# A hybrid decoder step on one core: the input projection of token blocks 2 to 4 in products of 512 columns

## The chip, the core and the metric

The kernel runs on one core of a Trainium2 chip. The time is the device time of one execution in microseconds, the median of three runs. The core has five engines that run side by side and meet through semaphores: TensorE (PE, matrix products; its loads of the stationary operand are shown apart as PEld), VectorE (DVE), ScalarE (ACT), GpSimd (POOL) and SyncE (SP), which here only issues DMA transfers. A product holds one operand of up to 128x128 still in the array (the stationary one) and streams the other through it (the moving one); its result goes to a bank of PSUM, which holds 512 float32 columns for each of 128 partitions.

## The reference

One inference step of a layer with two groups of heads, for 2048 new prompt tokens and 8 sequences of 8 sample tokens. All of them share one input projection:

```python
z = jnp.einsum('bsd,dc->bsc', x, w_in)            # 1024 x 3600
fq, fk, fv = z[..., 0:512], z[..., 512:1024], z[..., 1024:1536]   # attention: queries, keys, values
qk_in = z[..., OFF_M_QK:OFF_M_V]                  # 1024 columns, short convolution of width 4, then silu
mv, ig, lf = values, input gate, forget gate      # matrix memory (mLSTM)
og = jax.nn.sigmoid(z[..., OFF_M_O:] + b_og)      # 512 columns, output gate
```

Behind it come a causal attention with forgetting over the prompt, an attention of the sample tokens over 8192 cached positions, the chunked recurrence of the matrix memory, an output projection with layer norm, and a squared-ReLU network with a second layer norm. (The lines above shorten the reference's; the order of the columns is its own.)

## The kernel before

Everything is float32 and split: an operand `a` becomes `ah` (rounded by ScalarE, `split_hi`, L154) and `al = a - ah` (by VectorE, `split_lo`, L157), and one product becomes three, `ah*bh + ah*bl + al*bh`, in `mm3` (L163 to L165). So every step over 128 rows of the inner dimension issues three matmuls, each with its own weight load.

The work has four parts in order of time: A (input projection, `block_a`), B (prompt attention), O (output projection) and C (the network). Part A goes through four blocks of tokens, `BLKS`: block 1 holds the 64 sample tokens and 4 tiles of 128 prompt tokens, blocks 2 to 4 hold 4 tiles (512 tokens) each. In the code they are `bi` 0 to 3. For a block the split tokens lie in four tiles, `xh0`/`xl0` for the first 256 tokens (320 in block 1) and `xh1`/`xl1` for the other 256.

The columns come in passes of 256 (`W_PASSES`), 14 a block. `wload` fetches a pass in two pieces of 128x1024, each four row groups of 128 rows by 256 columns, and splits them (tiles `wra`, then `whi` and `wlo`, four buffers of each kind of split piece). The passes of a block, in their order:

- 2 passes `natural`: mLSTM values (and in the second one the gates `ig`, `lf`). The tokens are stationary, the 256 weight columns move; for each of the tiles 8 row groups x 3 matmuls go into one bank `pm`, then `sink` empties it.
- 4 passes for the convolution's input. Weights are stationary, 128 columns at a time (`j`), and 256 tokens move; for each half `i` of the block a bank, then a ScalarE copy into half of `qi`. After both halves VectorE does the convolution.
- 2 passes `natural`: output gates, stored as `dog`.
- 4 passes for the attention's queries and keys, in the manner of the convolution's input, stored as `dq` and `k_prompt`.
- 2 passes `natural`: the attention's values, stored as `v_prompt`. Their hooks also load the next block's tokens (`x_load`), split its first tile (`x_turn`), or in block 4 start loads for part B (`begin_b`).

Beside these passes two other streams are worked in. `tick(us)` is called behind each product with a share of time; each 2.3 units (`PACE_M`) let one step of the matrix memory through (`gate_stream`, `m_block`, `m_sample`; tiles `mr`, `mg`, `mm`, `mn`), each 5.6 units (`PACE_A`) one step of the sample attention (tiles `sQ`, `sO`, `sT`). A `natural` product ticks 2.6, a product with 256 moving tokens 2.56. The final order on each engine is set by a list scheduler that places instructions by its own estimate of when they become ready, so code order is not machine order. Buffers are released by the last instruction that uses a tile; within one tile, waits go by the region that is read or written.

Of the kernel before, what the change touches and what calls it, by code (L numbers as in the profile page):

```python
# [52 lines left out]
def body(ctx, tc, I, O, stages):  # L53
# [99 lines left out]
    def split_hi(dst, src, scale=1.0):  # L153
        last["ACT"] = A.activation(dst, src, AF.Copy, scale=scale)  # L154
# [141 lines left out]

    xT = {}
# [19 lines left out]
    def x_turn(bi, t):  # L317

        blk, pre, off = geom(bi)
        i = int(off[t] >= pre + 256)  # L320
        if len(xT.setdefault(bi, [])) == i:
            w = 256 if i else 320
            xT[bi].append((pa.tile([128, 8, w], F32R, name=f"xh{i}"), pa.tile([128, 8, w], F32R, name=f"xl{i}")))
        n = tok_n(t)
        xn = xns.pop(t)[:, :8 * n].rearrange("p (k c) -> p k c", k=8)
        (xh, xl), s = xcol(bi, t)
        split_hi(xh[:, :, s], xn)
        split_lo(xl[:, :, s], xn, xh[:, :, s])

    def xcol(bi, t):  # L330

        blk, pre, off = geom(bi)
        o = off[t]
        i = int(o >= pre + 256)
        o -= i * (pre + 256)
        return xT[bi][i], slice(o, o + tok_n(t))

# [120 lines left out]
    def block_a(bi):  # L458
# [3 lines left out]
        def natural(sink, *cols, hook=None, after=None):  # L462
            wh, wl = W0.pop() if W0 else wload(*cols)
            for i, t in enumerate(blk):
                if hook:
                    hook(i)
                m = tok_n(t)
                ps = ppa.tile([128, 512], F32, name="pm", tag="pm", bufs=4)[:m, :wh[0].shape[1]]
                (xh, xl), s = xcol(bi, t)
                for k in range(8):  # L470
                    mm3(ps, xh[:, k, s], xl[:, k, s], wh[k], wl[k], k == 0, k == 7)
                sink(t, m, ps)
                if after:
                    after(i)
                tick(2.6)

        def stage(ps, m, n):
# [26 lines left out]
        for j in range(8):  # L504
# [5 lines left out]
            if pre:  # L510
                qs = pa.tile([128, 8, 11], F32, name="qs", bufs=2)
                V.tensor_copy(qs[:, :, 0:3], scT[:, j])
            for i in range(2):
                xh, xl = xT[bi][i]
                w = 256 + (pre if i == 0 else 0)
                ps = ppa.tile([128, 512], F32, name="pm", tag="pm", bufs=4)[:, :w]
                for k in range(8):
                    mm3(ps, wh[k][:, cs], wl[k][:, cs], xh[:, k, :w], xl[:, k, :w], k == 0, k == 7)
                tick(w * 0.01)
                if w == 320:  # L520
                    A.copy(qs[:, :, 3:11], ps[:, 0:64].rearrange("p (b t) -> p b t", t=8))
                A.copy(qi[:, 3 + i * 256:259 + i * 256], ps[:, w - 256:])
            V.tensor_copy(hist[:, j], qi[:, 512:515])
# [25 lines left out]
        yield 1  # L549
        for i in range(2):  # L550
            def sink(t, m, ps, i=i):
# [10 lines left out]
        for j in range(8):  # L562
# [6 lines left out]
            scale = 1.0 if c else 0.125  # L569
            for i in range(2):  # L570
                xh, xl = xT[bi][i]
                w = 256 + (pre if i == 0 else 0)
                ps = ppa.tile([128, 512], F32, name="pm", tag="pm", bufs=4)[:, :w]
                for k in range(8):
                    mm3(ps, wh[k][:, cs], wl[k][:, cs], xh[:, k, :w], xl[:, k, :w], k == 0, k == 7)
                tick(w * 0.01)
                if w == 320:
                    for a in range(4):
                        V.tensor_scalar(qr[:, :, (j % 2) * 4 + a], ps[a * 32:a * 32 + 32, 0:64].rearrange("p (b t) -> p b t", t=8), scale, None, op0=OP.mult)
# [4 lines left out]
                st = pa.tile([128, 256], F32, name="st", bufs=4)  # L584
                A.activation(st, ps[:, w - 256:], AF.Copy, scale=scale)
                a = t0 + i * 256
                SY.dma_start(O["k_prompt"][jj * 128:(jj + 1) * 128, a:a + 256] if c else dq[jj, :, a:a + 256], st)
# [3 lines left out]
        for i in range(2):  # L591
            def sink(t, m, ps, i=i):
                d = v_out(t)[:, i * 256:(i + 1) * 256]
                (A if bi == 3 and i == 1 else SY).dma_start(d, stage(ps, m, 256))

# [7 lines left out]

            def b_first(n, i=i):
                if i == 1 and n == 0:
                    begin_b()
            natural(sink, (1024 + i * 256, 256), hook=b_first if bi == 3 else turn_first)

# [1394 lines left out]
```

## Time and profile before

| | us |
|---|---|
| median of 3 runs (3210.70 to 3214.76) | 3212.57 |
| profiled execution, its own time | 3215.55 |
| its span, first to last instruction | 3213.8 |
| part A, blocks 2 to 4, in the span | about 206 to 878 |
| part B begins | about 880 |
| granted TensorE clock, mean | 0.99 |

The page gives busy times of the engines, the span in 40 slices, DMA queues, the chain that ended last, and the costliest groups of instructions. In the groups, "mean ns of one" is the time from an instruction's start to its modelled end; matmuls overlap, so the distance from start to start is shorter, and it has to be read from the timeline.

### The profile page before, as it was taken

The numbers are of one execution on the slowest core, as the hardware profiler recorded it, in microseconds if no ns is written. First come the engines' busy times: TensorE is split into PE (matmuls) and PEld (weight loads), VectorE is DVE, ScalarE is ACT, GpSimd is POOL, SyncE is SP. The second block draws the span as 40 slices with busy tenths as digits, with TensorE's granted clock in tenths as the row PEclk, the third lists the DMA queues.
The fourth block names the chain that finished last, engine by engine and source line by source line (L and its number), as shares of the span: only waits on it lengthen the run. The fifth ranks groups of instructions, "written<-read, shape, count | busy, mean of one in ns | idle before, by whom it ended". The sixth has DMA issues, their size and how long they took to land. (4 is left out here: it accounts for less than half of the span.)

```text
span 3213.8 us, 57419 instructions
## 1 busy us (share of the span) xinstructions
PE 3124.1 (97%) x21597; PEld 2538.6 (79%) x21597; DVE 2082.2 (65%) x5046; ACT 1446.8 (45%) x2678; POOL 910.1 (28%) x973
## 2 busy tenths in 40 slices
PE   9999999999999999999999999999999999899998
PEld 8998998998867677677777777777767777698886
DVE  6856556465488788534556568556675665766667
ACT  4343344334378677412444445343444444344442
POOL 0121323423333333376333323334333211000000
PEclk9999999999999999999999999999999999999999
DMA  5565766867676866687887869878879866643231
GB/s 190 151 211 166 264 218 226 273 219 260 219 251 186 193 168 145 214 297 259 308 292 271 308 237 322 317 256 313 291 260 340 288 210 204 211 163 131 100 123 63
DMA packets 339340, 732.75 MB, mean 228 GB/s; under 512 B 63608, under 2 KB 177656, under 8 KB 338168
## 3 DMA queue, kind: packets, MB, share of 16 engines
q1 hardware_dynamic: 251928, 414.61, 39.8%
q0 software_dynamic: 83520, 304.12, 27.1%
q10 hardware_dynamic: 3616, 10.36, 0.9%
q8 instruction: 171, 2.80, 0.3%
q14 instruction: 105, 0.86, 0.1%
HBM read 676.13 MB, written 86.38 MB: 237 GB/s over the span
## 5 line engine op out<-in xcount | busy, mean ns | idle before, releaser
L157 DVE TENSOR_TENSOR wl<-wr,wh 128x1024 fp32r<-128x1024 f32 x300 | 365.7, 1222 | 246.1 <-ACT wh L154 207.1
L154 ACT ACTIVATE wh<-wr 128x1024 fp32r<-128x1024 f32 x300 | 315.4, 1055 | 330.7 <-PE py L165 140.0
L163 PE MATMUL ph<-x1h,wh 128*128 128x512 f32 (+1 forms) x1280 | 455.2, 356 | 0.0
L164 PE MATMUL ph<-x1l,wh 128*128 128x512 f32 (+1 forms) x1280 | 453.5, 354 | 0.2 <-DVE x1l L157 0.2
L165 PE MATMUL ph<-x1h,wl 128*128 128x512 f32 (+1 forms) x1280 | 451.5, 355 | 0.4 <-DVE wl L157 0.2
L1720 POOL DMA_INDIRECT kT<-cache_k,idxK x256 | 276.4, 1080 | 533.7 <-PE sQ L1743 468.6
L163 PE MATMUL py<-wh,hh 128*128 128x512 f32 x900 | 358.8, 403 | 10.4 <-DVE y L1369 6.4
L164 PE MATMUL py<-wl,hh 128*128 128x512 f32 x900 | 354.4, 395 | 0.7 <-issue 0.7
L165 PE MATMUL py<-wh,hl 128*128 128x512 f32 x900 | 351.9, 395 | 0.7 <-DVE hl L157 0.4
L1369 DVE TENSOR_TENSOR y<-y,py 128x512 f32<-128x512 f32 x410 | 276.8, 681 | 106.5 <-PE py L165 80.3
L163 PE MATMUL pm<-xh,whi 128*128 128x256 f32 (+1 forms) x1024 | 298.5, 292 | 0.0
L164 PE MATMUL pm<-xl,whi 128*128 128x256 f32 (+1 forms) x1024 | 294.5, 288 | 0.0
L165 PE MATMUL pm<-xh,wlo 128*128 128x256 f32 (+1 forms) x1024 | 293.6, 287 | 0.5 <-issue 0.5
L1831 POOL DMA_INDIRECT vt<-cache_v,idxV x164 | 179.1, 1092 | 386.8 <-PE sO L1855 315.1
L163 PEld LDWEIGHTS ph<-x1h,wh 128*128 128x128 f32 x1280 | 241.2, 188 | 40.2 <-issue 8.5
L165 PEld LDWEIGHTS ph<-x1h,wl 128*128 128x128 f32 x1280 | 240.6, 189 | 36.7 <-issue 3.7
L164 PEld LDWEIGHTS ph<-x1l,wh 128*128 128x128 f32 x1280 | 241.5, 189 | 35.0 <-issue 3.7
L163 PE MATMUL pm<-whi,xh 128*128 128x256 f32 (+2 forms) x816 | 237.0, 291 | 9.8 <-ACT whi L154 7.2
L164 PE MATMUL pm<-wlo,xh 128*128 128x256 f32 (+2 forms) x816 | 232.6, 285 | 0.8 <-DVE wlo L157 0.6
L165 PE MATMUL pm<-whi,xl 128*128 128x256 f32 (+2 forms) x816 | 232.3, 285 | 0.8 <-issue 0.8
L163 PEld LDWEIGHTS py<-wh,hh 128*128 128x128 f32 x900 | 169.4, 189 | 65.2 <-issue 25.1
L157 DVE TENSOR_TENSOR wlo<-wra,whi 128x1024 fp32r<-128x1024 f32 (+1 forms) x112 | 141.6, 1266 | 102.0 <-ACT whi L154 95.5
(364 smaller groups left out, 6806.7 us busy)
## 6 DMA issues: line engine op xcount, KB each, us to landing
wr<-w SPq DMA_DIRECT2D x200, 512.0 KB
wra<-w_in SPq DMA_DIRECT2D x104, 512.0 KB
wr<-dw SPq DMA_DIRECT2D x96, 512.0 KB
dw<-w POOLq DMA_DIRECT2D x48, 512.0 KB
Rb<-dR SPq DMA_DIRECT2D x128, 128.0 KB
kT<-dw SPq DMA_DIRECT2D x28, 512.0 KB
kT<-w SPq DMA_DIRECT2D x25, 512.0 KB
xn<-xp_t SPq DMA_DIRECT2D x16, 512.0 KB
```

The source lines that it names most:

```text
L154: last["ACT"] = A.activation(dst, src, AF.Copy, scale=scale)
L157: r = (eng or V).tensor_tensor(dst, src, hi.bitcast(F32), op=OP.subtract)
L163: T.matmul(ps, wh, xh, start=first, stop=False, skip_group_check=shared)
L164: T.matmul(ps, wh, xl, start=False, stop=False, skip_group_check=shared)
L165: last["PE"] = T.matmul(ps, wl, xh, start=False, stop=stop, skip_group_check=shared)
L1369: V.tensor_tensor(y, y, ps, op=op)
L1720: G.indirect_dma_start(out=piece(n), out_offset=None, in_=ck, in_offset=IO(ap=idxK[:, b, j // 2, j % 2:j % 2 + 1], axis=0))
L1831: vx["last"] = G.indirect_dma_start(out=vt.rearrange("p f c -> p (f c)"), out_offset=None, in_=cv, in_offset=IO(ap=idxV[:, b, (kt % 4) * 4 ...
```

## The change

Block 1 and the first two passes of each block stay. In blocks 2 to 4:

- The split tokens lie in one pair of tiles, `xh` and `xl` of 128x4608. In blocks 2 to 4 each token tile has its own 1024 columns (8 row groups x 128 tokens), so that for a row group the 512 tokens of a block are four runs of 128 at a distance of 1024. Block 1 keeps its two parts, inside the same pair of tiles (`xcol`, `xrun`).
- The convolution's input and the queries and keys take 512 moving tokens in one product and one bank, instead of twice 256 (`xrun`, `pv`). One ScalarE copy of 512 columns fills `qi`; queries and keys are still stored as two pieces of 256. Such a product ticks 5.12.
- Output gates and values go through `wide`: 512 columns, which are two former passes, move past each stationary token tile. The weights come in four pieces of two row groups x 512 columns (the same bytes, fetched as two runs of 512 numbers a partition). For each piece all four tiles are worked, each into its own bank, so all four banks `pm` stay in use over the pass and are emptied with the last piece. Each group of six matmuls ticks 1.3. The sinks work on 512 columns, in buffers shared with the convolution's `ac` and `qi`.
- The hooks of the values' pass move with it (`at`): the next block's first three token tiles are loaded behind the first group of pieces 0 to 2, its first tile is split behind the first group of the last piece; `begin_b` comes behind the first group of piece 2.

```diff
     def x_turn(bi, t):
-        blk, pre, off = geom(bi)
-        i = int(off[t] >= pre + 256)
-        if len(xT.setdefault(bi, [])) == i:
-            w = 256 if i else 320
-            xT[bi].append((pa.tile([128, 8, w], F32R, name=f"xh{i}"), pa.tile([128, 8, w], F32R, name=f"xl{i}")))
+        if not XX:
+            XX.extend(pa.tile([128, 4608], F32R, name=x) for x in ("xh", "xl"))
...
     def xcol(bi, t):
         blk, pre, off = geom(bi)
+        if bi:
+            o = off[t] * 8
+            return [X[:, o:o + 1024].rearrange("p (k c) -> p k c", k=8) for X in XX]
...
+    def xrun(bi):
+        if bi:
+            return [(512, [X[:, 0:4096].rearrange("p (t k c) -> p k t c", t=4, k=8) for X in XX])]
+        return [(w, [X[:, a:a + 8 * w].rearrange("p (k c) -> p k c", k=8) for X in XX]) for a, w in ((0, 320), (2560, 256))]
...
+        def wide(sink, c0, hook=None):
+            banks = [ppa.tile([128, 512], F32, name="pm", tag="pm", bufs=4) for _ in blk]
+            at0, at1 = (w_at[((c0 + i * 256, 256),)] for i in range(2))
+            for q in range(4):
+                wr = pa.tile([128, 4 * 272], F32, name="wra", bufs=2)[:, :1024]
+                SY.dma_start(wr.rearrange("p (s e) -> p s e", s=2),
+                             dap(I["w_in"], at0 + q // 2 * 131072 + q % 2 * 512, [[1024, 128], [at1 - at0, 2], [1, 512]]))
+                wh = pa.tile([128, 4 * 272], F32R, name="whi", bufs=4)[:, :1024]
+                wl = pa.tile([128, 4 * 272], F32R, name="wlo", bufs=4)[:, :1024]
+                split_hi(wh, wr)
+                split_lo(wl, wr, wh)
+                wh, wl = (x.rearrange("p (s k c) -> p k s c", s=2, k=2) for x in (wh, wl))
+                for i, t in enumerate(blk):
+                    xh, xl = xcol(bi, t)
+                    for k in range(2):
+                        mm3(banks[i].rearrange("p (s c) -> p s c", s=2), xh[:, 2 * q + k], xl[:, 2 * q + k], wh[:, k], wl[:, k],
+                            q == k == 0, q == 3 and k == 1)
+                    if hook:
+                        hook(q, i)
+                    if q == 3:
+                        st = (pa.tile([128, 512], F32, name="sa", tag="ac", bufs=2) if i % 2 else
+                              pa.tile([128, 512], F32, name="sq", tag="qi", bufs=2))
+                        sink(t, banks[i], st)
+                    tick(1.3)
...
-            for i in range(2):
-                xh, xl = xT[bi][i]
-                w = 256 + (pre if i == 0 else 0)
+            at = 3
+            for w, (xh, xl) in xrun(bi):
                 ps = ppa.tile([128, 512], F32, name="pm", tag="pm", bufs=4)[:, :w]
+                pv = ps.rearrange("p (t c) -> p t c", t=4) if w == 512 else ps
                 for k in range(8):
-                    mm3(ps, wh[k][:, cs], wl[k][:, cs], xh[:, k, :w], xl[:, k, :w], k == 0, k == 7)
+                    mm3(pv, wh[k][:, cs], wl[k][:, cs], xh[:, k], xl[:, k], k == 0, k == 7)
                 tick(w * 0.01)
...
+        def gate_out(t, ps, st):
+            V.tensor_tensor(st, ps, bog, op=OP.add)
+            A.activation(st, st, AF.Tanh, scale=0.5)
+            V.scalar_tensor_tensor(st, st, 1.0, nwh, op0=OP.add, op1=OP.mult)
+            SY.dma_start(dog[t * 128:t * 128 + 128], st)
+        if bi:
+            wide(gate_out, C_O)
+        for i in range(0 if bi else 2):
...
+        def v_store(t, ps, st):
+            A.copy(st, ps)
+            (A if bi == 3 else SY).dma_start(v_out(t), st)
+
+        def at(q, i):
+            if bi == 3:
+                if (q, i) == (2, 0):
+                    begin_b()
+            elif q < 3 and i == 0:
+                x_load(BLKS[bi + 1][q])
+            elif (q, i) == (3, 0):
+                x_turn(bi + 1, BLKS[bi + 1][0])
+                x_load(BLKS[bi + 1][3])
+
+        if bi:
+            wide(v_store, 1024, at)
+        for i in range(0 if bi else 2):
```

Three places show what becomes of the order of instructions. In each row the line is `mm3`'s or the helper's; L7xx to L19xx move by 56 lines between the two files.

The first is TensorE at the output gates of block 2. Before, one bank (`pm_4188`, tile 4's first 256 columns) is worked through all eight row groups, and the weights change under it after four:

```order
L163 MATMUL pm_4188<-whi_4178,xh0_2987 128x256
L164 MATMUL pm_4188<-wlo_4179,xh0_2987 128x256
L165 MATMUL pm_4188<-whi_4178,xl0_2988 128x256
L163 MATMUL pm_4188<-whi_4184,xh0_2987 128x256
L164 MATMUL pm_4188<-wlo_4185,xh0_2987 128x256
L165 MATMUL pm_4188<-whi_4184,xl0_2988 128x256
```

Now one piece of weights (`whi_3968`) stays and the banks go by under it (the transposition `mm_3781` belongs to the matrix memory of the sample tokens):

```order
L163 MATMUL pm_3964<-whi_3968,xh_147 128x512
L164 MATMUL pm_3964<-wlo_3969,xh_147 128x512
L165 MATMUL pm_3964<-whi_3968,xl_148 128x512
L890 MATMUL mm_3781<-ident_74,hT_3730 64x128
L163 MATMUL pm_3965<-whi_3968,xh_147 128x512
L164 MATMUL pm_3965<-wlo_3969,xh_147 128x512
L165 MATMUL pm_3965<-whi_3968,xl_148 128x512
```

What moved: a bank is left after six matmuls of 512 columns instead of 24 of 256, and the order of weights and tiles has changed places. In all, TensorE's program has 16,675 instructions, where it had 18,403.

The second is TensorE in block 3, where `m_block` takes two steps (each fills one `mn` with two heads) beside the queries' products. Before, each step stands alone between two products of 24 matmuls; this is the second one, the first stands 24 matmuls earlier:

```order
L165 MATMUL pm_7355<-xh1_5701,wlo_7205 128x256
L719 MATMUL mn_7380<-va_6908,Wm_6911 128x129
L720 MATMUL mn_7380<-Cs_5966,qa_6913 128x129
L719 MATMUL mn_7380<-va_6908,Wm_6911 128x129
L720 MATMUL mn_7380<-Cs_5966,qa_6913 128x129
L163 MATMUL pm_7407<-xh0_5623,whi_7397 128x256
```

Now both steps stand side by side behind one product (and a step of the sample attention, `sO`, in the second of them):

```order
L775 MATMUL mn_6329<-va_6030,Wm_6033 128x129
L776 MATMUL mn_6329<-Cs_5316,qa_6035 128x129
L775 MATMUL mn_6340<-va_6030,Wm_6033 128x129
L776 MATMUL mn_6340<-Cs_5316,qa_6035 128x129
L775 MATMUL mn_6340<-va_6030,Wm_6033 128x129
L1911 MATMUL sO_5877<-vt_6111,PTs_5742 32x256 x4
L1911 MATMUL sO_5877<-vt_6109,PTs_5742 32x256 x4
L776 MATMUL mn_6340<-Cs_5316,qa_6035 128x129
L163 MATMUL pm_6379<-xh_147,whi_6369 128x512
```

What moved: a product ticks 5.12 at once, and two steps of 2.3 go through together. The numbers of steps are the same in both: 336 `sQ`, 170 `sO` and 62 `sT` matmul instructions stand ahead of part B in either program.

The third is the SP queue at the end of the values' pass of block 2. Before, stores of 256 columns stand between the fetches of weights (`wra`):

```order
L284 DMA wra<-w_in 128x1024
L594 DMA v_prompt<-st 128x256
L656 DMA Wm<-dM 128x4x128
L656 DMA qa<-dar 128x4x128
L594 DMA v_prompt<-st 128x256
L1727 DMA Rb<-dR 128x1x256 x2
L594 DMA v_prompt<-st 128x256
L664 DMA va<-dv 128x4x128
L704 DMA og<-dog 128x512
L594 DMA v_prompt<-st 128x256
L284 DMA wra<-w_in 128x1088 x2
```

Now:

```order
L284 DMA wra<-w_in 128x1088
L712 DMA Wm<-dM 128x4x128
L712 DMA qa<-dar 128x4x128
L284 DMA wra<-w_in 128x1024
L315 DMA xn<-xp_t 128x1024
L637 DMA v_prompt<-sq 128x512
L720 DMA va<-dv 128x4x128
L637 DMA v_prompt<-sa 128x512
L637 DMA v_prompt<-sq 128x512
L760 DMA og<-dog 128x512
L637 DMA v_prompt<-sa 128x512
```

What moved: the next pass's weights and the next block's last token tile (`xn`) stand ahead of all the stores, and there are four stores of 512 columns, all at the end.

More of the change, by code (lines that the diff above doesn't have):

```diff
@@ L521, in block_a @@
                     A.copy(qs[:, :, 3:11], ps[:, 0:64].rearrange("p (b t) -> p b t", t=8))
-                A.copy(qi[:, 3 + i * 256:259 + i * 256], ps[:, w - 256:])
+                n = w // 256 * 256
+                A.copy(qi[:, at:at + n], ps[:, w - n:])
+                at += n
             V.tensor_copy(hist[:, j], qi[:, 512:515])
@@ L583, in block_a @@
                         SY.dma_start(O["k_sample"][jj * 128:(jj + 1) * 128], st)
[L584 to L587, printed above, removed]
+                for o in range(w % 256, w, 256):
+                    st = pa.tile([128, 256], F32, name="st", bufs=4)
+                    A.activation(st, ps[:, o:o + 256], AF.Copy, scale=scale)
+                    SY.dma_start(O["k_prompt"][jj * 128:(jj + 1) * 128, a:a + 256] if c else dq[jj, :, a:a + 256], st)
+                    a += 256
             if pre and j % 2 == 1:
@@ L590, in block_a @@
         kx["new"] = True
-        for i in range(2):
+        def v_store(t, ps, st):
[13 more added lines that the diff above has]
+        for i in range(0 if bi else 2):
             def sink(t, m, ps, i=i):
-                d = v_out(t)[:, i * 256:(i + 1) * 256]
-                (A if bi == 3 and i == 1 else SY).dma_start(d, stage(ps, m, 256))
+                SY.dma_start(v_out(t)[:, i * 256:(i + 1) * 256], stage(ps, m, 256))
             def turn_first(n, i=i):
@@ L602, in turn_first @@
                     x_load(BLKS[bi + 1][3])
[L604 to L607, printed above, removed]
+            natural(sink, (1024 + i * 256, 256), hook=turn_first)
     dgs_s = drm.tile([4, 8], F32, name="dgs_s")
```

33 lines of the change are left out of this document (16 added, 17 removed).

## The prediction

> **What bounds the kernel now.** I read the page's engine rows first, then the stretch of blocks 2 to 4 in a view by windows, then TensorE's waits in it, then the timeline for the distance between matmuls.
>
> ```profile
> span 3213.8 us, 57419 instructions
> PE 3124.1 (97%) x21597; PEld 2538.6 (79%) x21597; DVE 2082.2 (65%) x5046; ACT 1446.8 (45%) x2678; POOL 910.1 (28%) x973
> 206.00:878.00 672.00, 661.54 (x5949) 616.05 (x5947) 381.28 (x1086) 251.38 (x536) 202.88 (x215) 1.00 0.69 229
> 206.00:878.00 672.00, 536.35 (x4187) 1.00 0.69 229
> PE sO L1855 <- DMA vt<-cache_v,idxV: 3.2, 2, 2.7
> PE sT L1792 <- ACT PTs L1814: 1.5, 1, 1.5
> PE pm L165 <- issue: 1.3, 3, 0.6
> PE sT L1812 <- ACT PTn L1794: 1.2, 1, 1.2
> PE mm L634 <- POOL va L663: 0.9, 1, 0.9
> ```
>
> TensorE is busy 97% of the span. In the stretch of blocks 2 to 4 (first window row: length, then busy time of PE, PEld, DVE, ACT, POOL, then granted clock, DMA share, GB/s) it is busy 661.54 of 672 us at clock 1.00; 536.35 us of that belong to the projection's products `pm` (second window row, `pm` alone). VectorE has 381 us and ScalarE 251 us, so neither bounds. The waits of TensorE there (us in total, times, longest) sum to some 8 us. So a change of this stretch is worth what it takes from TensorE's own stream.
>
> **What a matmul costs, narrow and wide.** A start-to-start distance is what counts. Two pieces of the timeline (start, duration), the first with 256 moving columns behind a step of the sample attention, the second in part C with 512 behind such a step:
>
> ```profile
> 857.11 1.05 PE L1855 MATMUL sO<-vt,PTs 128*32 128x256 f32 x16
> 858.08 0.39 PE L163 MATMUL pm<-whi,xh 128*128 128x256 f32 x1
> 858.31 0.28 PE L164 MATMUL pm<-wlo,xh 128*128 128x256 f32 x1
> ...
> 859.38 0.28 PE L164 MATMUL pm<-wlo,xh 128*128 128x256 f32 x1
> 1645.68 1.05 PE L1855 MATMUL sO<-vt,PTs 128*32 128x256 f32 x16
> 1646.66 0.50 PE L163 MATMUL py<-wh,hh 128*128 128x512 f32 x1
> 1647.00 0.40 PE L164 MATMUL py<-wl,hh 128*128 128x512 f32 x1
> ...
> 1649.10 0.39 PE L164 MATMUL py<-wl,hh 128*128 128x512 f32 x1
> ...
> 1657.26 0.39 PE L164 MATMUL py<-wl,hh 128*128 128x512 f32 x1
> 1649.00:1657.00 8.00, 8.00 (x37) 1.00 0.97 331
> 412.92 0.28 PE L164 MATMUL pm<-wlo,xh 128*128 128x256 f32 x1
> ...
> 415.44 0.28 PE L164 MATMUL pm<-wlo,xh 128*128 128x256 f32 x1
> ```
>
> Undisturbed: from 412.92 to 415.44 lie 21 steps (every third row is L164), 2.52/21 = 0.120 us for 256 columns. From 1649.10 to 1657.26 lie 36 steps (a multiple of three; the window counts 37 that touch its 8 us), 8.16/36 = 0.227 us for 512 columns. Two narrow ones take 0.240, so each pair that becomes one wide matmul saves 0.013 us. The columns take the same time either way; what goes is a fixed share of one matmul.
>
> The Trainium skill, "TensorE: Matmul & The Clock Gate", section "Back-to-back issue gap", gives a warm gap of N/2.4 + 2.5 ns, that is a fixed share of 2.5 ns; by it, as an estimate, the fixed share would save 1728 x 0.0025 = 4 us and the sum would be a loss of some 3 us. The trace doesn't agree: 0.120 us above, where the formula gives 0.109.
>
> Behind an interruption the first ten steps are dearer. Narrow: 858.08 to 859.38 is 1.30 us for ten, 0.10 over 1.20. Wide: 1646.66 to 1649.10 is 2.44 us, 0.17 over 2.27. So each entry costs 0.07 us more when the products are wide.
>
> **The sum.** Per block, 8 x 24 wide matmuls for the convolution's input, 96 for gates, 8 x 24 for queries and keys, 96 for values: 576, in three blocks 1728, where there were 3456.
>
> - Fixed share: 1728 x 0.013 = 22.5 us saved, all on TensorE and so on the path.
> - Entries: the built order has 98 places in blocks 2 to 4 where another stream's work is followed by a wide product; 98 x 0.07 = 6.9 us lost. (No cost if the entry were like the narrow one.)
> - Fewer interruptions: 109 entries into products where the order before has 123, since two matrix-memory steps now go together; 14 x 0.10 = 1.4 us saved.
> - Instruction supply: TensorE waits 1.3 us on "issue" at `pm` in these blocks, and now has 1728 matmuls and loads fewer to fetch. Worth 0 to 1.3; I take 0, since the quoted wait is 3 single cases.
> - Steps side by side: two steps of `m_block` with no product between them give VectorE, ScalarE and POOL less cover. Some 20 such pairs stand in the new order. The nearest row is the wait of `mm` on POOL, 0.9 us, once in 12 chunks before. Bounds 0 and 10 x 0.9 = 9 us, if every second pair waited like that; I take 1.5, since most pairs use buffers freed a product (5.4 us) earlier.
>
> 22.5 - 6.9 + 1.4 - 1.5 = 15.5 us. Against the profiled execution's 3215.55 us that is 3200; that one lies 3 us above the median, and against the median it is 3197.
>
> **What I cost at nothing, and its cover.**
>
> ```profile
> L157 DVE TENSOR_TENSOR wlo<-wra,whi 128x1024 fp32r<-128x1024 f32 x104 | 130.9, 1261 | 93.3 <-ACT whi L154 86.9 <-PE mn L720 2.7 <-PE pm L165 2.1
> L154 ACT ACTIVATE whi<-wra 128x1024 fp32r<-128x1024 f32 x104 | 109.0, 1057 | 82.9 <-PE pm L165 23.9 <-PE pm L164 23.2 <-DMA wra<-w_in 21.5
> L522 ACT COPY qi<-pm 128x256 f32<-128x256 f32 x64 | 22.8, 368 | 67.1 <-PE pm L165 59.3 <-DVE qk L535 3.2 <-remote 3.1
> L555 DVE TENSOR_TENSOR st<-pm,bog 128x256 f32<-128x256 f32 x32 | 13.3, 415 | 12.9 <-remote 4.8 <-PE pm L165 3.1 <-issue 2.7
> ```
>
> A weight piece in `wide` needs ScalarE 1.06 and VectorE 1.26 us and covers 24 matmuls, 5.45 us; four buffers let the splits run ahead, and a buffer is now free after each piece. Without that cover a piece would stop TensorE for 2.3 us. The fetch brings the same bytes in runs half as long; between the release of a buffer and the use of its next filling, the order leaves at least 4.3 us of products (3.8 before), by the distances above. Token tiles: the next block's first tile is split behind the first group of the last piece, with three groups (4.1 us) for 2.3 us of splitting; its readers in the old block are then done. Emptying a bank: twice 0.37 us (L522) or twice 0.42 (L555) become at most 0.84 in one; a bank is used again at least 4 us later. On SP, weights and token tiles are queued ahead of the stores, and the four wide stores end with the pass; `og` waits for `dog`, which is now complete only 4 us before the next product, but its use lies several steps on. POOL's gathers keep their number and order, with 2 to 3% less time between them: 3.2 us of waits on `vt` could become 5. At the change to part B the last `pm` matmul is still what VectorE's last state update waits for; the larger ScalarE copy adds 0.25 us beside that.
>
> **Rivals.**
>
> *The moving operand in runs costs.* Tokens now come in four runs of 128 (1152 matmuls), weights in two of 256 (576). If each of the 1152 x 3 + 576 = 4032 breaks cost as much as the fixed share of a matmul, 0.013 us, that would be 52 us, and the time 3212.6 + 52 - 15.5 = 3249. It decides from 15.5/4032 = 0.004 us a break. Against it:
>
> ```profile
> 855.36 1.93 PE L1743 MATMUL sQ<-kT,qb 128*32 128x256 f32 x32
> ```
>
> `sQ` moves two runs of 128, `sO` (the rows at 857.11 and 858.08 above) one of 256: from 855.36 to 857.11 it is 1.75/32 = 0.055 us a record, then 0.97/16 = 0.061 us. A break costs nothing there; it is plain float32 in a narrow array, so this isn't proof. 6%.
>
> *The waits take it.* Pairs of steps, gathers and the token splits stop TensorE for 9 us more than I allow: 3206 or a little over. For it: POOL and SP work in order, and one late gather holds `hh` and so the transposition. Against it: only 8 us of waits in 672 before. 12%.
>
> *Part B falls out otherwise.* The scheduler orders part B anew, though no line of it changes: TensorE's order differs from its first products on.
>
> ```profile
> PE pt L1019 <- ACT PT L1022: 5.8, 3, 3.0
> PE pS L974 <- DVE mx L982: 1.9, 3, 0.8
> 878.00:900.00 22.00, 15.92 (x72) 0.69 0.77 208
> ```
>
> Its waits sum to some 15 us from 880 to 1420, most in few places; one of 3 us more or less, at either sign, is within reach, and one low-clock window like the one at its begin (0.69 over 22 us) costs some 5. As a mechanism that alone gives no more than 3192 or 3203. 4% that it takes the time out of the range.
>
> *The clock gives way.* `wide` changes its bank every six matmuls of 512. If the granted clock sank to 0.69 there, as at the change to part B, 6 passes of 21.8 us would take 59 us more: 3256. But `py` in part C changes among its four banks every six matmuls of 512 too, and its window above has clock 1.00. The Trainium skill, "TensorE: Matmul & The Clock Gate", section "A second HAM failure mode: psum-queue depth-cycling", speaks of such oscillation at 512 columns with banks changing; by that rule this rival would hold, and the trace of part C doesn't agree. 2%.
>
> That the change would not do what it says is excluded: 1728 fewer TensorE instructions stand in the program.
>
> **How the numbers follow.** Forecast 76%, waits 12%, runs 6%, part B 4%, clock 2%. The likeliest case gives 3197. Its bounds: entries as before, no new wait and issue gained give 22.5 + 1.4 + 1.3 = 25, 3187; 9 us of waits in place of 1.5 give 3205, and part B's 3 us beside that 3207 or 3208. The range 3187 to 3207 holds the forecast and some of the waits' case. 0.2% is 6.4 us, about what a measurement can tell: faster means under 3206.1. The forecast, part B and half of the waits' case lie there, 86%; the other half of the waits' case is no change, 6%; runs and clock are slower, 8%.
>
> **What would show it.** In the changed profile, wide `pm` matmuls 0.227 us apart, blocks 2 to 4 shorter by about 15 us, the same clock, TensorE's waits there near 10 us, the distance behind an entry as in part C. Wrong if the distance of `pm` with four runs is over 0.231, if `mn`, `mm` or `sO` wait for tens of us, or if part B alone moves by more than 5 us.

## The result, and the profile after

The changed kernel is slower: 3227.42 us against 3215.0 us for the kernel before on the same chip (medians of 10 runs each), a ratio of 1.0045 with a 95% interval of 1.0034 to 1.0055. The forecast was 3197 us, some 15 us faster. So about 30 us are to be explained. The profiled execution took 3224.22 us, 3 us under its median; against the 3200 that were forecast for it, 24 us are to be explained there.

The page of the changed kernel, its span and engine rows:

```profile
span 3222.5 us, 53779 instructions
...
PE 3107.6 (96%) x19869; PEld 2444.2 (76%) x19869; DVE 2082.1 (65%) x5022; ACT 1439.0 (45%) x2630; POOL 906.0 (28%) x973
```

TensorE is 16.5 us less busy than before (3124.1), in a span 8.7 us longer. Where the time went is read from two windows of each kernel: from 200 us, inside the end of block 1, to the first product of part B (`pS`), and from there to the end. Columns: length, then busy time of PE, PEld, DVE, ACT, POOL, then clock, DMA share and GB/s. The kernel before:

```profile
200.00:880.40 680.40, 668.31 (x6003) 622.46 (x6002) 385.45 (x1096) 254.48 (x544) 207.00 (x222) 1.00 0.69 228
880.40:3213.80 2333.40, 2268.73 (x14146) 1731.98 (x14146) 1546.21 (x3462) 1117.60 (x1978) 676.26 (x712) 0.99 0.69 232
```

The changed kernel:

```profile
200.00:888.50 688.50, 661.70 (x4275) 532.24 (x4274) 382.80 (x1073) 245.95 (x500) 201.53 (x219) 0.99 0.67 225
888.50:3222.50 2334.00, 2258.68 (x14146) 1727.60 (x14146) 1549.96 (x3462) 1119.75 (x1978) 677.61 (x714) 0.99 0.69 232
```

Part B and what follows is as long as before (2334.0 against 2333.4), though TensorE is 10.0 us less busy in it and idle for 10.6 us longer; so of the 16.5 us only 6.6 lie in part A. The whole difference lies in part A, which is 8.1 us longer. There TensorE's idle time (length less busy) went from 12.1 to 26.8 us, and its busy time fell by the 6.6.

The idle time by what ended it, 206 to 888.5 us of the changed kernel (total, times, longest):

```profile
PE sO L1911 <- DMA vt<-cache_v,idxV: 6.0, 2, 4.4
PE sT L1868 <- ACT PTs L1870: 3.4, 1, 3.4
PE mm L690 <- POOL va L719: 3.1, 1, 3.1
PE mm L690 <- POOL hh L685: 3.0, 2, 1.8
PE mr L385 <- DVE rows L392: 1.9, 1, 1.9
PE mm L752 <- ACT hh L707: 1.8, 1, 1.8
PE mm L690 <- DVE hh L685: 1.6, 1, 1.6
PE sQ L1799 <- DMA kT<-cache_k,idxK: 1.5, 2, 1.3
PE mn L775 <- DVE Wm L755: 1.3, 1, 1.3
```

Of the products `pm`, none waits for its weights or bank, and one for its tokens (0.4 us, in a row further down). All else that waits are steps of the two streams beside the projection: matrix memory (`mm`, `mn`, `mr`) and sample attention (`sO`, `sT`, `sQ`), for nine different reasons.

The products themselves. TensorE's timeline of the changed kernel, output gates of block 2 (weights move in two runs of 256) and keys of block 3 (tokens move in four runs of 128):

```profile
323.22 1.12 PE L907 MATMUL mm<-vx,kws 64*128 64x512 f32 x2
324.27 0.50 PE L164 MATMUL pm<-wlo,xh 128*128 128x512 f32 x1
...
326.68 0.39 PE L165 MATMUL pm<-whi,xl 128*128 128x512 f32 x1
...
327.36 0.39 PE L165 MATMUL pm<-whi,xl 128*128 128x512 f32 x1
...
330.54 0.39 PE L164 MATMUL pm<-wlo,xh 128*128 128x512 f32 x1
...
609.00 0.39 PE L165 MATMUL pm<-xh,wlo 128*128 128x512 f32 x1
...
612.40 0.40 PE L165 MATMUL pm<-xh,wlo 128*128 128x512 f32 x1
```

From 327.36 to 330.54 lie 14 steps, 3.18/14 = 0.227 us. From 609.00 to 612.40 lie 15, 3.40/15 = 0.227. Both are what part C showed before, so runs in the moving operand cost nothing. The granted clock stays at 1.00 while the banks change, here in two stretches of the gates' passes (length, busy time of PE, clock, DMA share, GB/s):

```profile
318.00:344.00 26.00, 26.00 (x119) 1.00 0.65 204
530.00:556.00 26.00, 26.00 (x163) 1.00 0.52 169
```

Behind the step at 323.22 the first ten distances sum to 2.41 us, 0.14 over 2.27; over all 98 entries into wide products the mean is 0.12 (without those behind a long wait), against 0.08 for all 132 entries before.

And a cost that was in none of the terms. The changed kernel's TensorE around the wait of 3.1 us:

```profile
415.50 0.39 PE L163 MATMUL pm<-whi,xh 128*128 128x512 f32 x1
419.02 0.87 PE L690 MATMUL mm<-ident,hh 128*128 128x128 f32 x4 [3.13 <-POOL va L719]
419.55 0.78 PE L164 MATMUL pm<-wlo,xh 128*128 128x512 f32 x1
...
420.55 0.63 PE L163 MATMUL pm<-whi,xh 128*128 128x512 f32 x1
420.98 0.63 PE L164 MATMUL pm<-wlo,xh 128*128 128x512 f32 x1
...
422.95 0.40 PE L163 MATMUL pm<-whi,xh 128*128 128x512 f32 x1
423.19 0.39 PE L164 MATMUL pm<-wlo,xh 128*128 128x512 f32 x1
```

Behind the wait the distance is 0.43 us instead of 0.227, for some 3 us, and then normal again; in the trace's clock record the granted clock is 0.50 there. The same stands behind the waits of 3.4 us (at 649) and 4.4 us (at 816). Together the products lose 5.6 us to it; the kernel before has no such stretch in these blocks.

Summed from the distances between all matmuls of these blocks (from 206 us to `pS`), each distance put down to the matmul that begins it: products -12.6 us (5.6 of low clock in it), steps among themselves +7.4 (25 of their matmuls ran at the low clock, which is about 1.6 of it; more of them stand directly behind one another, since a product follows a step only 118 times instead of 132; how the rest divides is open), idle +13.5, the rest -0.2. That is +8.1.

### The profile page after: what moved, and what is told of

Same layout as the page of the kernel before. It is cut to its first block, busy times and chain, and to the rows that moved or that the text cites. A ratio compares the mean times of both kernels' runs of the same rounds, so it can differ in the third digit from the quotient of the medians.

```text
span 3222.5 us, 53779 instructions
## 1 busy us (share of the span) xinstructions
PE 3107.6 (96%) x19869; PEld 2444.2 (76%) x19869; DVE 2082.1 (65%) x5022; ACT 1439.0 (45%) x2630; POOL 906.0 (28%) x973
## 5 line engine op out<-in xcount | busy, mean ns | idle before, releaser
L163 PE MATMUL pm<-xh,whi 128*128 128x512 f32 (+2 forms) x640 | 231.1, 361 | 0.0
L165 PE MATMUL pm<-xh,wlo 128*128 128x512 f32 (+2 forms) x640 | 228.7, 357 | 0.0
L164 PE MATMUL pm<-xl,whi 128*128 128x512 f32 (+2 forms) x640 | 227.2, 355 | 0.0
L163 PE MATMUL pm<-whi,xh 128*128 128x256 f32 (+4 forms) x624 | 203.5, 327 | 10.8 <-ACT whi L154 7.9
L164 PE MATMUL pm<-wlo,xh 128*128 128x256 f32 (+4 forms) x624 | 201.1, 322 | 0.6 <-DVE wlo L157 0.6
L165 PE MATMUL pm<-whi,xl 128*128 128x256 f32 (+4 forms) x624 | 201.2, 323 | 0.4 <-DVE xl L157 0.4
```

What stands on the lines that cost most here:

```text
L163: T.matmul(ps, wh, xh, start=first, stop=False, skip_group_check=shared)
L164: T.matmul(ps, wh, xl, start=False, stop=False, skip_group_check=shared)
L165: last["PE"] = T.matmul(ps, wl, xh, start=False, stop=stop, skip_group_check=shared)
```

## The experiments

Each ratio is to the kernel before on the same chip, by 10 runs (8 for one), with its 95% interval. "Idle" is TensorE's idle time from 200 us to `pS` in the one profiled execution. One execution can lie up to 8 us off its kernel's median, so idle times are compared in groups. Distances, entries and the low clock are summed from the timeline and the trace's clock record.

### Which part of the change

Only the convolution's input and the queries and keys wide; output gates and values as before:

```diff
-        if bi:
-            wide(gate_out, C_O)
-        for i in range(0 if bi else 2):
+        for i in range(2):
...
-        if bi:
-            wide(v_store, 1024, at)
-        for i in range(0 if bi else 2):
+        for i in range(2):
```

> Only the convolution's input and the queries and keys are wide (1152 wide products); output gates and values are as before. TensorE's own stream: 1152 x 0.013 = 15 us saved, some 70 entries x 0.07 = 5 us lost. Three theories of the 15 us of new waits. Bunched steps (two steps of the matrix memory behind one product of 5.4 us): the waits of these passes stay, some 13 us, so -15 + 5 + 13 = +3 us, ratio 1.001. Passes `wide` (finer ticks, weights and token tiles ahead of the stores): the waits go, -10 us, ratio 0.997. Cover (the streams beside the products need their time, and whatever TensorE saves becomes waiting): about 0, ratio 1.000, with waits up by some 10 us.

Measured: 1.0012 (0.9999 to 1.0026). Its window:

```profile
200.00:885.30 685.30, 662.31 (x4863) 562.29 (x4862) 386.46 (x1097) 251.70 (x524) 206.25 (x222) 0.99 0.69 227
```

Idle 23.0 us, 12.9 of it in five waits of `sO` for a gather.

Only output gates and values wide:

```diff
-            return [(512, [X[:, 0:4096].rearrange("p (t k c) -> p k t c", t=4, k=8) for X in XX])]
+            return [(256, [X[:, o:o + 2048].rearrange("p (t k c) -> p k t c", t=2, k=8) for X in XX]) for o in (0, 2048)]
```

> Only output gates and values go through `wide` (576 wide products); the convolution's input, queries and keys are in halves of 256 tokens (two runs of 128) with ticks of 2.56. 576 x 0.013 = 7.5 us saved, some 28 entries x 0.07 = 2 us lost. Bunched steps: no new waits, -5.5 us, ratio 0.998. Passes `wide`: the waits in the values' pass and just behind it stay, some 16 us, so +10 us, ratio 1.003. Cover: about 0, ratio 1.000.

Measured: 0.9982 (0.9969 to 0.9995), 5.8 us faster, which is what its own terms gave.

```profile
200.00:871.90 671.90, 663.93 (x5418) 589.84 (x5416) 381.62 (x1072) 251.96 (x522) 211.73 (x219) 1.00 0.69 231
```

Idle 8.0 us. So `wide` alone, with its pieces of two row groups, its late stores and its four banks, is not what waits. The two parts alone would add up to about -1.9 us (+3.9 - 5.8); together they cost 14.

Only the queries and keys in halves, all else wide:

```diff
-            for w, (xh, xl) in xrun(bi):
+            for w, (xh, xl) in xrun(bi, 2):     # the queries' and keys' loop: two parts of 256 tokens
```

> The changed kernel with the attention's queries and keys alone in halves of 256 tokens with ticks of 2.56; the convolution's input stays wide, and output gates and values stay in `wide`. 1152 wide products save 15 us, some 60 entries cost 4 us. If the waits come with the wide queries and keys (where the wait for `vt` at 800 to 820 us stands in all three kernels that have them wide): waits as before, -11 us, ratio 0.9965. If they come with any product that ticks 5.12: half of them stay, -3 us, 0.999. Chance: 0.995 to 1.003.

Measured: 1.0005 (0.9989 to 1.0022), idle 672.30 - 658.39 = 13.9 us. Part A was 8 us shorter than in the kernel before, but what follows 6 us longer in this execution. Neither of the two clear answers came out; the ratio lies in the range that was given to chance.

### Steps in pairs, or TensorE's speed

A tick of 2.56 in the middle of a wide product and one at its end:

```diff
                     mm3(pv, wh[k][:, cs], wl[k][:, cs], xh[:, k], xl[:, k], k == 0, k == 7)
-                tick(w * 0.01)
+                    if w == 512 and k == 3:
+                        tick(2.56)
+                tick(2.56 if w == 512 else w * 0.01)
```

> The changed kernel, but a product of 512 tokens ticks 2.56 behind its fourth row group and 2.56 at its end, so that steps no longer stand in pairs. Some 25 more entries cost 25 x 0.17 = 4 us. Bunched steps: most of the 15 us of new waits go, some 9 us below the changed kernel, ratio 1.001 to before. Passes `wide`: the waits stay, ratio 1.006. Cover: the waits stay, ratio 1.005.

Measured: 1.0013 (1.0003 to 1.0023), 10 us better than the changed kernel, as the theory of pairs had forecast.

```profile
200.00:877.00 677.00, 660.03 (x4260) 529.42 (x4258) 385.55 (x1072) 244.53 (x491) 205.66 (x218) 0.99 0.69 228
```

Idle 17.0 us, in the fastest of its ten runs. But the edit undid only part of the pairs: the two `mn` steps of a chunk still start within 1.1 us of each other in six of the twelve chunks of these blocks, in the changed kernel in nine, in the kernel before in two. So the tick of 5.12 is not alone what puts steps side by side, and this run can't tell pairs from another order. The next kernel speaks against the theory of pairs. It keeps the ticks of the changed kernel and issues each product of 512 columns as two of 256:

```diff
+    def mm6(ps, wh, wl, xh, xl, first, stop):
+        a = [slice(0, ps.shape[1] // 2), slice(ps.shape[1] // 2, ps.shape[1])]
+        for w, x, f, s in ((wh, xh, first, False), (wh, xl, False, False), (wl, xh, False, stop)):
+            for h in a:
+                last["PE"] = T.matmul(ps[:, h], w, x[:, h], start=f, stop=s, skip_group_check=True)
```

(All instructions are issued, but each half opens the bank anew, so the sums lack the opening product of the first half.)

> The changed kernel with each product of 512 columns issued as two of 256 with the same stationary operand, so that the 22 us of fixed share come back on TensorE and 7 us of dear entries go, while passes, pieces, ticks and stores are those of the changed kernel. Bunched steps and passes `wide`: the waits are of the structure and stay, so 15 us above the changed kernel, ratio 1.008 to before. Cover: with TensorE slow again the waits fall to those of before (13 us), ratio 1.001.

Measured: 0.9993 (0.998 to 1.0006).

```profile
200.00:883.50 683.50, 672.78 (x6007) 625.99 (x6006) 380.43 (x1073) 246.51 (x498) 204.47 (x219) 1.00 0.69 227
```

Idle 10.7 us, with the steps in pairs nearly as in the changed kernel, in eight of the twelve chunks. So pairs alone don't make the waits; they come when TensorE is also faster. The scheduler has ordered this kernel anew too, so one such run is not enough; a second order follows below.

### GpSimd's queue

The longest wait, at 816 us, shows one way in which they come. GpSimd in the changed kernel:

```profile
798.45 1.05 POOL L681 TENSOR_TENSOR r<-r,nhalf 128x4 f32<-128x4 f32 x1 [21.52 <-DVE r L680]
803.74 0.64 POOL L745 TENSOR_SCALAR_AFFINE_SELECT Wm<-Wm 128x512 f32<-128x512 f32 x1 [4.24 <-ACT Wm L744]
804.35 1.27 POOL L747 TENSOR_TENSOR qa<-qa,qk 128x512 f32<-128x512 f32 x1
...
805.72 1.28 POOL L685 TENSOR_TENSOR hh<-hh,og 128x512 f32<-128x512 f32 x1
807.18 1.05 POOL L1887 DMA_INDIRECT vt<-cache_v,idxV  x1 [0.17 <-issue]
808.53 0.95 POOL L1887 DMA_INDIRECT vt<-cache_v,idxV  x1 [0.30 <-PE pm L165]
```

And in the kernel before, the same chunk:

```profile
800.91 1.05 POOL L625 TENSOR_TENSOR r<-r,nhalf 128x4 f32<-128x4 f32 x1 [5.58 <-DVE r L624]
803.19 1.29 POOL L629 TENSOR_TENSOR hh<-hh,og 128x512 f32<-128x512 f32 x1 [1.23 <-DVE hh L627]
...
804.68 1.03 POOL L1831 DMA_INDIRECT vt<-cache_v,idxV  x1 [0.16 <-issue]
806.01 0.96 POOL L1831 DMA_INDIRECT vt<-cache_v,idxV  x1 [0.30 <-issue]
806.99 0.64 POOL L689 TENSOR_SCALAR_AFFINE_SELECT Wm<-Wm 128x512 f32<-128x512 f32 x1
```

Before, the gathers stand ahead of the next chunk's `Wm`. Now they stand behind it, and `Wm` waits for ScalarE, which waits for a load. SP, ScalarE and TensorE in the changed kernel's timeline:

```profile
796.10 0.40 SPq L712 DMA_DIRECT2D Wm<-dM  x1
...
802.39 1.28 ACT L744 ACTIVATE Wm<-Wm,gm 128x128 f32<-128x128 f32 x4 [4.77 <-DMA Wm<-dM]
...
816.16 1.93 PE L1911 MATMUL sO<-vt,PTs 128*32 128x256 f32 x16 [4.38 <-DMA vt<-cache_v,idxV]
```

From the issue of the load to ScalarE's start it is 6.3 us. `hh` and the gathers are held up behind it, and `sO` begins 7.6 us after the second gather was issued. In the kernel before the same load and the same step of ScalarE lie 8.1 us apart, but `hh` and the gathers stand ahead of them on GpSimd:

```profile
796.87 0.38 SPq L656 DMA_DIRECT2D Wm<-dM  x1
...
805.00 1.28 ACT L688 ACTIVATE Wm<-Wm,gm 128x128 f32<-128x128 f32 x4 [3.23 <-DMA Wm<-dM]
```

To test this, the attention's step was put ahead of the matrix memory's in `tick`:

```diff
     def tick(us):
+        acc[0] += us
+        while acc[1] is not None and acc[0] > acc[2]:
+            acc[0] -= acc[2]
+            attend()
         macc[0] += us
...
-        acc[0] += us
-        while acc[1] is not None and acc[0] > acc[2]:
-            acc[0] -= acc[2]
-            attend()
```

> The changed kernel with the two streams of a tick in the other order in the code: the sample attention's step ahead of the matrix memory's, so that a gather of `vt` stands ahead of the next chunk's work on GpSimd. Theory GpSimd's queue (the gathers and `hh` stand behind `Wm`, `qa`, `wkc`, which wait for a load): the waits of `sO` on `vt`, 6.3 us, and the low clock behind them, 2 us, go, so 6 to 8 us below the changed kernel, ratio 1.002 to before. Theory spacing (the steps in pairs are what waits): no change, 1.0045. Theory chance (any other order gives another set of waits): anywhere from 0.999 to 1.007.

Measured: 1.0058 (1.0041 to 1.0074). Idle 698.40 - 664.60 = 33.8 us; the waits for gathers stayed (7.6 us, the longest 5.2), so the edit did not move what it was meant to move: in its trace GpSimd still issues the gathers at 817.60 and 818.95, behind the `Wm` at 814.15. It says nothing for or against this theory.

The product of `hh` and `og` on VectorE:

```diff
-                    norm_out(hh, 128, og, t0, V if c == 15 else None)
+                    norm_out(hh, 128, og, t0, V)
```

> The changed kernel with the product of `hh` and `og` on VectorE in place of GpSimd for all chunks. Theory GpSimd's queue: the waits of the transposition `mm` on GpSimd (6.6 us in the changed kernel) and the low clock behind the longest, 1.4 us, go; 12 products of 1.3 us come onto VectorE, which is busy 56% of part A, and cost nothing. 8 us below the changed kernel, ratio 1.002 to before. Theory spacing: another engine's wait takes their place, 1.0045. Theory chance: 0.999 to 1.007.

Measured: 1.001 (0.9994 to 1.0026), 11 us better than the changed kernel. Idle 676.20 - 656.42 = 19.8 us. The waits of `mm` on GpSimd went, as expected, but those on VectorE's `hh` rose from 1.6 to 3.9 us. The same edit in the kernel before:

> The kernel before with the product of `hh` and `og` on VectorE. If GpSimd's queue is what the change made worse: little to win here (0.9 us of waits on GpSimd), ratio 1.000 within 0.001. If it is chance: off 1 by 0.002 or more at either sign.

Measured: 1.0011 (0.9999 to 1.0022), nothing won over all runs. In its profiled execution, 7.5 us under the median, the idle time is the least of all:

```profile
200.00:873.10 673.10, 667.72 (x6010) 623.11 (x6009) 394.93 (x1110) 256.20 (x546) 191.06 (x210) 1.00 0.70 231
```

That is 5.4 us, where the changed kernel with the same edit has 19.8. And both helpful edits in the changed kernel together:

> The changed kernel with ticks of 2.56 in the middle and at the end of a product of 512 tokens, and with the product of `hh` and `og` on VectorE. Alone these gave 10 us each against the changed kernel. If they take away different waits (spacing and GpSimd's queue each for itself): 8 us below the kernel before, ratio 0.9975. If both only found another order: no sum, 0.9985 to 1.003.

Measured: 0.9991 (0.9975 to 1.0007), idle 675.00 - 657.51 = 17.5 us. The gains did not quite add up (-10 and -11 us alone, -17 together). The ratio lies where the second answer has it, but its interval reaches the first; it is not measurably different from the kernel before.

### The order of the steps

If many unlike edits each give some 10 us, the order itself may be what is drawn anew. The only edit here is the constant that says how often a matrix-memory step is let through:

```diff
-PACE_M = 2.3
+PACE_M = 2.35
```

> The kernel before with the share of one step of the matrix memory 2.35 in place of 2.3, so that the order of the steps changes and no work does. Theory chance: the waits of TensorE in part A move by 5 us or more, ratio off 1 by 0.002 or more, to either side. Theories spacing and GpSimd's queue: single steps between narrow products as before, waits within 3 us of before, ratio within 0.001 of 1.

Measured, in the kernel before: 1.0035 (1.0018 to 1.0051), 11 us slower with no change of work. Its idle time from 200 us hardly moved (12.8 us), so of the theory of chance the ratio came true and the waits did not; part A ended 7.5 us later and the rest was 9 us longer, in one execution. So a kernel's time depends on the order of these steps by nearly as much as this change was to bring, and 2.3 is a good value for the kernel before. Then the same for other values, in both kernels:

> The changed kernel with a matrix-memory step each 2.4 units in place of 2.3: no work changes, the order does. Theory chance (the waits are those of one order among many, and the kernel before sits at a good one, since 2.35 in it costs 11 us): ratio to before between 0.998 and 1.006, waits in part A between 15 and 35 us. Theory structure (products of 512 columns with these ticks wait in any order): waits near 30 us again, ratio 1.003 to 1.006.

> The changed kernel with 2.2 in place of 2.3. As for 2.4: by chance anywhere from 0.998 to 1.006 with waits of 15 to 35 us; by structure 1.003 to 1.006 with waits near 30.

> The kernel before with a matrix-memory step each 2.2 units. Chance: ratio to before 1.001 to 1.005, as at 2.35, so that the changed kernel at 2.2 (1.003) is not slower than its partner. Structure: within 0.001 of 1, and the changed kernel at 2.2 is the slower one by 0.2% or more.

> The kernel before with 2.4. Chance: 1.001 to 1.005, so that the changed kernel at 2.4 (0.9982) is the faster one by 10 us or more, near the 19 us of its own stream (fixed share less entries). Structure: 0.996 or less, faster than the changed kernel at 2.4.

> The changed kernel with 2.5. If 2.4 is one good order among many (chance): 1.000 to 1.005. If the wide products want fewer steps each (two ticks of 5.12 hold four steps at 2.5 too, but fewer stand in threes): again 0.998 or less.

| units a step | before: ratio | before: idle, us | changed: ratio | changed: idle, us |
|---|---|---|---|---|
| 2.2 | 1.0016 (1.0002 to 1.003) | 15.9 | 1.003 (1.0014 to 1.0046) | 22.9 |
| 2.3 | 1 | 12.1 | 1.0045 (1.0034 to 1.0055) | 26.8 |
| 2.35 | 1.0035 (1.0018 to 1.0051) | 12.8 | | |
| 2.4 | 1.0016 (1.0 to 1.0031) | 17.0 | 0.9982 (0.9971 to 0.9993) | 19.3 |
| 2.5 | | | 1.003 (1.0016 to 1.0043) | 29.5 |

The windows behind the idle times of the changed kernel at 2.4 and of the kernel before at 2.4:

```profile
200.00:876.70 676.70, 657.45 (x4288) 532.05 (x4287) 382.15 (x1075) 246.58 (x500) 208.29 (x221) 0.99 0.69 230
```

```profile
200.00:892.10 692.10, 675.09 (x6007) 627.58 (x6005) 390.82 (x1099) 256.33 (x548) 203.24 (x223) 0.99 0.69 225
```

Two things follow. The changed kernel at 2.4 is 0.18% faster than the kernel before at 2.3, and 0.6% faster than itself at 2.3: the order is worth more than the change. And the idle time is not only order: 12 to 17 us in four orders with narrow products, 19 to 30 in four with wide ones. Over the three common values the mean ratios are 1.0011 and 1.0019, so the change as a whole cannot be told from no change there.

The variant with only output gates and values wide was tried at 2.4 too:

> Only output gates and values wide, with 2.4. At 2.3 this gave 0.9982. Own stream 5.5 us below before. Chance: 0.996 to 1.002 with waits in part A between 8 and 20 us. If 2.4 suits the steps in any kernel: 0.996 or less.

Measured: 1.0006 (0.9994 to 1.0018), idle 683.00 - 669.30 = 13.7 us (8.0 at 2.3). So its gain at 2.3 was also in part its order.

### Pairs or speed, in a second order

The mid-product ticks and the halves at 2.4:

> The changed kernel with ticks of 2.56 in the middle and at the end of a product, at 2.4 units a step. Own stream some 16 us below the kernel before. Spacing: waits in part A as in the kernel before, 14 to 19 us, and 0.996 to 0.999 to before. Cover: waits of 20 us or more, and 0.999 to 1.003.

Measured: 1.0012 (0.9998 to 1.0026).

```profile
200.00:886.50 686.50, 661.98 (x4272) 532.98 (x4272) 385.40 (x1075) 245.98 (x499) 205.87 (x221) 0.98 0.69 226
```

> The changed kernel with each product of 512 columns issued as two of 256, at 2.4 units a step: the fixed share is back, the ticks are those of the changed kernel. Spacing: waits in part A of 22 to 33 us, as in the changed kernel at four paces. Cover: 14 to 19 us, as in the kernel before, and 0.999 to 1.002.

Measured: 1.0026 (1.0011 to 1.0042), a little over the 0.999 to 1.002 that the theory of cover gave.

```profile
200.00:888.40 688.40, 672.42 (x5995) 625.20 (x5994) 380.09 (x1072) 244.94 (x494) 204.81 (x221) 0.99 0.69 225
```

Idle 24.5 us with ticks of 2.56 and wide products, 16.0 with ticks of 5.12 and halves (10.7 at 2.3); the `mn` steps stand in pairs in seven of the twelve chunks in either. So what the ticks gave in the first order is gone in the second, and the halves twice have the idle time of narrow kernels. By the profiles without other edits: six with every product narrow (the kernel before at four values, the halves at two) 10.7 to 17.0, mean 14.1; four of the changed kernel 19.3 to 29.5, mean 24.6; two with mid-product ticks 17.0 and 24.5. With `hh` on VectorE it is 5.4 narrow and 19.8 wide. So with the faster TensorE the steps wait some 10 us more, out of the 17 that it gains on its own stream; pairs alone don't do that. This rests on groups of single executions, which touch at 17.0. The half clock comes on top: by the clock record, part A from 200 us has 10 to 19 us of it in the changed kernel at the four values, and 0 to 10 in the kernel before.

## Why the prediction was wrong, point by point

- **Fixed share (22.5 us saved): right.** Wide products run 0.227 us apart on both operands' layouts. The products' distances fell by 12.6 us; with the low clock taken out, 18.2. The terms on TensorE's own stream gave 22.5 - 6.9 + 1.4 = 17.0.
- **Entries (6.9 us lost): right in kind, too high.** 98 entries, as counted; 0.12 us each where I took 0.17, and 0.08 before where I took 0.10. One entry in part C had been taken for all.
- **Instruction supply (0, bounds 0 and 1.3): the upper bound came true.** No `pm` waits on "issue" in the changed kernel's list, where the kernel before has 1.3 us of it; with the halves at 2.3 such waits of `pm` are back with 1.6 us.
- **Steps side by side (1.5 us, bounds 0 and 9): the step that failed.** Idle time rose by 14.7 us in this order and by some 10 over several. The bound was worked out from one row, the wait of `mm` on GpSimd, times a number of pairs. But nine kinds of wait grew, `sO` and `sQ` on gathers, `sT` on ScalarE, `mr` on VectorE, and the kernels with nearly as many pairs but narrow products wait only 10.7 and 16.0 us in all. What fits is that the streams beside the products have chains of their own, such as the 6.3 us from the issue of `Wm`'s load to ScalarE's start on it, and that the products are their cover, which became shorter; this chain was followed for one wait, not for all nine. I looked at the cover of weights, tokens and banks, which held but for 0.4 us, and for the streams I wrote only that 2 to 3% less time lies between the gathers, with 5 us of waits on `vt` (6.0 came).
- **The steps' own distances: in no term.** They take 7.4 us more, about 1.6 of it at half clock.
- **Clock: right for the wide products, wrong behind waits.** They change banks at clock 1.00. But the products lost 5.6 us at half clock behind three waits of over 3 us; no term had that, and the rivals had a low clock only for the changing banks and at the start of part B.
- **Part B (no change): right in its length,** 2334.0 against 2333.4 us, with less busy and more idle time in it.
- **The rivals.** Runs in the moving operand cost nothing (0.227 us). "The waits take it" was the one that came true, with its place (one late gather, `hh`, the transposition) but priced at 9 us, so it ended at no change; waits and low clock together were 20 (14.7 and 5.6).
- **The sign** hung on one thing more that no term had: the kernel before sits at the best of its four measured orders, the changed one at 2.3 at the worst of its four. Over several orders my estimate of the change is about nothing: 17 us gained, less 10 of waits and up to 5 of half clock (half of the 10 us by which its stretches are longer on average). The mean ratios at the three common values differ by 0.0008, some 3 us. So that it came out slower by as much as 12 us was in part the draw. A change that lets a scheduler order everything anew gives a good order up.

What stays open is which property of an order makes it good. The idle time from 200 us does not tell it alone: at 2.35 the kernel before is 11 us slower with 12.8 us of idle time, and the halves at 2.4 are 8 us slower with 16.0. At 2.35 the traces show where the time lies, though not why: from the start of the span to `pS` TensorE is idle for 28.9 us instead of 25.1 and busy for 859.0 instead of 855.3, and behind `pS` the clock record has 78 us of half clock instead of 65.

## What to carry to other kernels

A saving on the bound engine's own stream is worth what is left after the streams worked in beside it have lost that cover: list their chains, how long each takes and the engine that each waits on, and give that loss a bound of its own, up to the saving itself. Where a constant sets how those streams are interleaved, measure a change at several values of it in both versions; here one value said +0.45% and another -0.18%, and the kernel before moved by 0.35%. Of these versions the changed kernel at 2.4 and the one with only output gates and values wide at 2.3 were the fastest (both 0.9982).

## What the runs showed of the hardware

Half clock follows many waits of TensorE of over 2 us, but not all of them. In part A from 200 us on, over the twenty profiles here, 18 of the 19 waits over 3 us have a stretch of clock 0.50 within 1.5 us of their end; so have more than half of the 28 waits between 2 and 3 us, and 3 of the 26 between 1.5 and 2 us. Behind the wait of 2.4 us in the kernel with `hh` on VectorE (at 463.6) nine narrow products stand 0.23 us apart, and behind its wait of 3.0 us (at 705.6) wide ones 0.43; its wait of 2.8 us (at 437.5) and the kernel before's of 2.7 us (at 539.1) are followed by none. A stretch is 3.4 us long in the clock record, or two or three times that. The Trainium skill, "TensorE: Matmul & The Clock Gate", section "HAM oscillation — how this bites in real kernels", puts the bound for idle gaps at about 3.4 us; here shorter ones were enough, and the measurement decides. In the changed kernel the three waits concerned, 11.0 us in all, cost the products 5.6 us more, about half as much again.
